# A delta net's block inverse issued in one row on VectorE, with low parts of weights moved to GpSimd meanwhile

## The chip, the cores and the metric

The kernel runs on one core of a Trainium2 chip. A core has TensorE (matmuls, with a queue of weight loads of its own), VectorE, ScalarE, GpSimd, and SyncE, which issues most of the DMAs. In the profile's rows they are PE, PEld, DVE, ACT, POOL and SP. The metric is the time of one execution on the device in microseconds (us).

## The reference

The reference is a trunk of four blocks on a sequence of 1024 tokens of 1024 features: a gated delta net, a feed-forward block with a convolution, a retention, and a second feed-forward block. Only the delta net is touched. Cut to what matters here, it is:

```python
proj = h @ w_in                                   # q, k, v, z, a, b
qkv = silu(causal_dwconv(qkv, conv_w))            # 4 taps
q, k, v = chunks of 64 tokens, 8 heads of 128     # q and k normalised
kk = where(strict, (k * beta) @ k.T * decay, 0)
sol = solve_triangular(kk + eye, [v * beta, k * beta * exp(gc)])
qk = where(causal, q @ k.T * decay, 0)
# a scan over the chunks: state and output from sol, q, k, qk
o = o * rsqrt(mean(o * o) + eps) * norm_w * silu(z)
return o @ w_out
```

The kernel treats two chunks of 64 as one chunk of 128 tokens, 8 of them, and computes the inverse of `kk + eye` for each head and chunk instead of a solve: first of its diagonal blocks of 32x32, then by matmuls of larger blocks.

## The kernel before, in words

**The stage.** The delta net's features, inverses and scan lie at about 90 to 658 us of the span. A generator per job issues its instructions: `filler` (L1028), `t_front`, `t_solve` (L766), `t_chain`, `prep`, `dt_half` (L911) and `scan`. The planner `run` (L627) holds a model clock `clk` that each matmul advances by its cost, and always resumes the job of the best priority among those that are due. A job yields a number (it is due so many us later; the numbers are in the table `LAT`), or the name of an event that another job announces with `emit`. TensorE's matmuls and transposes (`pm`, `ptr`, L616 and L619) are pinned to the order in which the planner issues them. On the other engines the framework orders the instructions from the priorities in which they were issued and from when their inputs and buffers are ready by its own model; the result is one fixed queue per engine.

**The filler.** It has the last priority and keeps TensorE busy. For each 128 columns of the projection it loads a weight tile (128x1024, 512 KB) with `load_w` (L100): a DMA brings `wr`, ScalarE copies it to the rounded high part `wh` (L89), and `split` subtracts that to get the low part `wl` (L90, on VectorE). Then come 48 matmuls of 128x512, 24 for each half of the sequence, and in each group of three the first one reads `wl`. There are two buffers each for `wr`, `wh` and `wl`; the two of `wr` are shared with `mvw`, the tiles of background products for later blocks (`bg_step`, `bg_ada`, L214 and L216, VectorE multiply-adds of 128x512). `conv_half` (L424) takes a projection from PSUM: ScalarE copies it to `raw` (L430) and scales it into `qkv` (L433), VectorE adds three taps (L435), ScalarE applies the silu (L436).

**The solve.** `t_solve` is done twice, for heads 0 to 3 and for heads 4 to 7. ScalarE gathers the 32x32 blocks to `X` (L773), VectorE transposes them to `Y` (L777), GpSimd sets `T` (L779, L780), and 31 steps follow, each a product into `fs` (L785) and a subtraction on `T` (L787), every one needing the one before it. Then VectorE transposes `T` to `RX` (L791), ScalarE permutes it to `TP` (L793), and VectorE transposes that to `TX` (L795). `t_chain` copies diagonal blocks out of these: `R` from `RX`, 12 copies on ScalarE (L833) and 12 on GpSimd (L835) for the two pairs of heads, and `T0` from `TX` on ScalarE (L822, 6 copies per pair of heads), and then multiplies blocks on TensorE. `dt_half` loads the decay into `DT`, multiplies q and k on TensorE in PSUM tiles named `mm`, and VectorE multiplies both (L933).

**Numbers of lines.** In the kernel after, lines from 434 on are moved by one or more: the low part stays L90, the projection is L617, the taps L436, the silu L437, the inverse L786 and L788, `RX` L790, `TP` L792, `TX` L794, the copies to `R` L835 and L837, and to `T0` L824.

Of the kernel before, what the change touches and what calls it, by code (L numbers as in the profile page):

```python
# [12 lines left out]
ALU = mybir.AluOpType  # L13
# [3 lines left out]
D = 1024  # L17
# [4 lines left out]
GH = 8  # L22
# [11 lines left out]
def trunk_kernel(ctx: ExitStack, tc, A):  # L34
    nc = tc.nc
    pe, act, dve, pool, sp = nc.tensor, nc.scalar, nc.vector, nc.gpsimd, nc.sync
# [24 lines left out]
    def mm_tile():  # L61
        return ps.tile([P, HALF], F32, tag="mm", name="mm", bufs=2)

    def sc_tile():
        return ps.tile([P, HALF], F32, tag="sc", name="sc", bufs=2)
# [26 lines left out]
    anchor = {}  # L92

    def after(key):
        return tc.issue_after(anchor[key].ins) if key in anchor else nullcontext()
# [4 lines left out]
    def load_w(src, tags=("wh", "wl"), raw="wr", eng=dve):  # L100
        wr = tl(raw, [P, D])
        anchor["w"] = sp.dma_start(wr, src)
        wh = tl(tags[0], [P, D], F32R, name="wh")
        wl = tl(tags[1], [P, D], F32R, name="wl")
        split(wh, wl, wr, eng)
        return kn(wh), kn(wl)
# [12 lines left out]
    def bg_step(tile=mm_tile):  # L119
        bg_ps[0] = tile  # L120
        if bg:
            bg.pop(0)()
# [38 lines left out]
    for k in range(KT):  # L161
        w = two("hTa", F32, "mvw")
# [261 lines left out]
    def conv_half(tile_idx, acc, half, o, prev):  # L424
        raw = tl("cv", [P, 516], name="raw")
        if half == 0:
            pool.memset(raw[:, 0:3], 0.0)
        else:
            pool.tensor_copy(raw[:, 0:3], prev[:, HALF:HALF + 3])
        act.activation(raw[:, 3:515], acc, AF.Copy)  # L430
        w = gdn_cw[:, tile_idx * 4:tile_idx * 4 + 4]
        oh = o[half]
        act.activation(oh, acc, AF.Copy, scale=w[:, 3:4])  # L433
        for j in range(1, 4):
            dve.scalar_tensor_tensor(oh, raw[:, 3 - j:515 - j], w[:, 3 - j:4 - j], oh, ALU.mult, ALU.add)  # L435
        act.activation(oh, oh, AF.Silu)  # L436
        return raw  # L437

# [3 lines left out]
    def ssq_tile(ti, tr):  # L442
        o = feats[ti]
        r = ssq[ti] = ct(f"ssq{ti}", [P, NCH])
        for half in range(2):
            pt = acc_tile()
            sq = tl("cv", [P, 516], name="sq")
            for c in range(4):
                cs = slice(c * P, (c + 1) * P)
                tr(pt[:, cs], o[half][:, cs])  # L450
            for c in range(4):
                n = half * 4 + c
                cs = slice(c * P, (c + 1) * P)
                act.activation(sq[:, cs], pt[:, cs], AF.Square, accum_out=r[:, n:n + 1])
        if ti < GH:
            dve.tensor_scalar(r, r, 1e-6, 1e-6 * P, ALU.add, ALU.mult)
        else:
            dve.tensor_scalar(r, r, 1e-6, None, ALU.add)
# [162 lines left out]
    def after_ev(*names):  # L621
        return ("ev", names)

    def emit(name, lat=0.0):
        events[name] = clk[0] + lat
# [50 lines left out]
    def give(tag, n):  # L676
        free[tag] += n
# [88 lines left out]
    def t_solve(qd_):  # L766
        yield after_ev(("T0", 2 * qd_ - 1), ("A", 2 * qd_), ("A", 2 * qd_ + 1))
        yield from take("lane", 1)
        X = tl("lane", [P, 32, 32], name="X")
        for h in pairs[2 * qd_] + pairs[2 * qd_ + 1]:  # L770
            for b in range(4):
                bs = slice(32 * b, 32 * b + 32)
                act.activation(X[bs, :, h % 4 * 8:h % 4 * 8 + 8].rearrange("p i c -> p c i"), U[h][bs, :, bs], AF.Copy)  # L773
        yield from take("lane", 2)
        yield LAT["X"]
        Y = tl("lane", [P, 32, 32], name="Y")
        dve.transpose(flat(Y), flat(X))  # L777
        T = tl("lane", [P, 32, 32], name="T")
        pool.memset(T, 0.0)  # L779
        pool.memset(flat(T)[:, 0:1024:33], 1.0)  # L780
        tmp = tl("fs", [P, 256], name="fs")
        for j in range(31):
            ni, nj = 31 - j, j + 1
            tv = tmp[:, 0:ni * nj].rearrange("p (i j) -> p i j", j=nj)
            dve.tensor_tensor(tv, bc(Y[:, j + 1:, j], nj), bm(T[:, j, 0:nj], ni), ALU.mult)  # L785
            ts_ = T[:, j + 1:, 0:nj]  # L786
            dve.tensor_tensor(ts_, ts_, tv, ALU.subtract)  # L787
            if j % 2:  # L788
                yield LAT["fs"]
        RX = tl("lane", [P, 32, 32], name="RX")  # L790
        dve.transpose(flat(RX), flat(T))  # L791
        TP = tl("lane", [P, 32, 32], name="TP")  # L792
        act.activation(TP, T.rearrange("p i j -> p j i"), AF.Copy)  # L793
        TX = tl("lane", [P, 32, 32], name="TX")  # L794
        dve.transpose(flat(TX), flat(TP))  # L795
        RTX[qd_] = (RX, TX)
        give("lane", 1)
        emit(("Tq", qd_))
        emit(("T", qd_), LAT["T"])
# [111 lines left out]
    def dt_half(p, q4):  # L911
        heads = pairs[p]
        if q4 == 0:
            yield after_ev(("Tq", p // 2), ("M", p - 1))
            yield from take("lane", 1)
            t = tl("lane", [P, 2, HALF], name="DT")
            tiles = [t[:, 0], t[:, 1]]
        else:
            yield after_ev(("Tq", p // 2), ("S", p - 1))
            yield from take("auh", 2)  # L920
            emit(("Dt", p))
            tiles = [tl("auh", [P, HALF], name="DT") for _ in range(2)]
        for h, t in zip(heads, tiles):
            DT[h, q4] = t
            sp.dma_start(t, Ld[h][:, hs(q4)])
        yield LAT["ld"]
        for h, t in zip(heads, tiles):
            yield after_ev(("f", h))
            pt = mm_tile()
            for c in range(4):  # L930
                n = q4 * 4 + c
                pm(pt[:, c * P:(c + 1) * P], fx(GH + h, n), fx(h, n))
            dve.tensor_tensor(t, t, pt, ALU.mult)  # L933
            emit(("D", h, q4), LAT["D"])
            yield LAT["mm"]
# [84 lines left out]
    kept = {}  # L1020
    zd = dr.tile([GH, P, S], F32, tag="zd", name="zd")

    def ssq_late(ti):
        yield LAT["ssq"]
        ssq_tile(ti, ptr)
        emit(("f", ti), 1.0)

    def filler(items):  # L1028
        spare = [(z, k) for k in range(GH)]
        todo = list(items)  # L1030
        while todo or spare:
            if not todo or (todo[0][0] == "c" and free["qkv"] < 2 and len(spare) > 4):
                kind, ti = spare.pop(0)
            else:
                kind, ti = todo.pop(0)
            if kind == "h":
                if ti > 1:
                    acc = acc_tile()
                    for k in range(KT):
                        mm3(acc, ws[ti], k, hT[1][k], k == 0, k == KT - 1, pm)  # L1040
                        yield 0.0
                    first_out(ti, 1, acc)
                if first[ti] < GH:
                    yield [(0.2, ssq_late(first[ti]))]
                else:
                    emit(("f", first[ti]), LAT["fv"])
                continue
            w = load_w(A["gdn_wqkv" if kind == "c" else "gdn_wz"][ti])
            prev = None
            if kind == "c":  # L1050
                feats[ti] = []
            for half in range(2):
                if kind == "c":
                    yield from take("qkv", 1)
                acc = acc_tile()
                for k in range(KT):
                    mm3(acc, w, k, hT[half][k], k == 0, k == KT - 1, pm)
                    yield 0.0
                if kind == "c":
                    feats[ti].append(tl("qkv", [P, HALF], name="qkv"))  # L1060
                    prev = conv_half(ti, acc, half, feats[ti], prev)
                else:
                    cv = tl("cv", [P, 516], name="sg")
                    act.activation(cv[:, 0:HALF], acc, AF.Silu)  # L1064
                    act.dma_start(zd[ti, :, hs(half)], cv[:, 0:HALF])
            if kind == "c":
                if ti < GH:
                    yield [(0.2, ssq_late(ti))]
                else:
                    emit(("f", ti), LAT["fv"])  # L1070
            bg_step(acc_tile)

    LAT = {"kk": 3.05, "ld": 1.14, "g1": 17.30, "gm": 2.50, "mm": 1.81, "T": 4.98, "X": 3.38, "fs": 1.9, "T0": 5.00, "t1": 1.65, "t2": 2.35, "t3": 1.34, "D": 2.67, "s1": 1.60, "s2": 1.22, "s3": 1.26, "tail": 12.31, "ssq": 9.30, "fv": 2.85}
    pairs = [(2 * p, 2 * p + 1) for p in range(GH // 2)]
    for nm in ("S", "T0", "Dt", "M", "Tq"):
        events[nm, -1] = 0.0
# [848 lines left out]
```

## Time and profile before

| | us |
|---|---|
| median of three runs | 3008.86 |
| the three runs | 3005.67, 3008.86, 3013.61 |
| profiled execution | 3004.66 |
| its span | 3002.8 |
| TensorE busy | 2834.6 (94%) |
| VectorE busy | 2197.4 (73%) |
| ScalarE busy | 1348.8 (45%) |
| GpSimd busy | 604.6 (20%) |

The span is the time that the trace of the profiled execution covers; its mean granted TensorE clock is 0.979 of full speed. In a row of the timeline the first number is the start in us from the beginning of the span, the second the duration of the instructions named, and the brackets at the end hold the idle time in front of them and what ended it. A row of grouped instructions ends in their count, the sum of their time in us, the mean of one in ns, and the idle time in front of them.

### The profile page before, as it was taken

How to read it: one execution, taken by the hardware profiler on the slowest of the kernel's cores; microseconds unless marked ns; L12 is line 12 of the kernel's file. 1: busy time of each engine (PE TensorE's matmuls, PEld its weight loads, DVE VectorE, ACT ScalarE, POOL GpSimd, SP SyncE). 2: the span in 40 equal slices, each digit the busy share in tenths (PEclk: the TensorE clock that was granted, in tenths of full speed). 3: DMA queues.
4: the chain of work that ended last, by engine and by line, in shares of the span. 5: the costliest groups of instructions: out<-in, count | busy, mean ns of one | idle time of the engine just before them, and what ended most of it. 6: DMA issues, size and time to landing. Idle time of an engine off the chain costs nothing.

```text
span 3002.8 us, 38880 instructions
## 1 busy us (share of the span) xinstructions
PE 2834.6 (94%) x13638; PEld 2307.8 (77%) x13638; DVE 2197.4 (73%) x3877; ACT 1348.8 (45%) x2513; POOL 604.6 (20%) x629
## 2 busy tenths in 40 slices
PE   8889998999989999999999989999999899999997
PEld 7768877887778788777787777767777678888785
DVE  5785687545687888997677765666687787778888
ACT  4655555434644444536443332221345544445444
POOL 0410311133011111620002330322201011113503
PEclk9999999999999999999999999999999999999998
DMA  7222222344344444864424463556663233336652
GB/s 272 88 75 71 95 88 64 117 158 137 109 140 161 161 155 147 305 203 127 154 82 147 158 216 110 166 169 184 197 235 129 99 133 106 105 106 216 230 172 105
DMA packets 235379, 442.35 MB, mean 147 GB/s; under 512 B 22192, under 2 KB 75696, under 8 KB 235184
## 3 DMA queue, kind: packets, MB, share of 16 engines
q1 hardware_dynamic: 205024, 387.96, 39.2%
q10 hardware_dynamic: 25152, 34.61, 3.2%
q0 software_dynamic: 5008, 17.30, 1.5%
q8 instruction: 107, 1.75, 0.2%
q14 instruction: 88, 0.72, 0.1%
HBM read 331.26 MB, written 108.53 MB: 146 GB/s over the span
## 4 chain that ended last, share of the span: by engine, by line
PE 61%; DVE 16%; issue 9%; DMA 7%; ACT 4%; POOL 2%; SPq 0%; POOLq 0%; ACTq 0%; DVEq 0%
PE acc L616 15%; PE acc L1401 7%; PE acc L1138 7%; PE acc L110 4%; PE acc L111 4%; PE acc L112 4%; PE sc L616 4%; PE sc L1138 3%; PE mm L616 2%; PE sc L1401 2%; DVE ab L90 1%; DVE bb L90 1%; PE sc L111 1%; PE sc L110 1%; PE sc L112 1%
## 5 line engine op out<-in xcount | busy, mean ns | idle before, releaser
L1401 PE MATMUL acc<-bb,ab 128*128 128x512 f32 x1800 | 431.9, 393 | 7.7 <-DVE bb L90 5.6
L1401 PEld LDWEIGHTS acc<-bb,ab 128*128 128x128 f32 x1800 | 337.3, 189 | 84.3 <-DVE bb L90 9.8
L616 PE MATMUL acc<-hT,wh 128*128 128x512 f32 x960 | 302.4, 396 | 0.0
L1539 POOL TENSOR_TENSOR o<-o 128x512 f32<-128x512 f32 x88 | 118.6, 1359 | 720.7 <-DVE o L1532 713.8
L1138 PE MATMUL acc<-T,wb 128*128 128x512 f32 x840 | 207.5, 397 | 12.5 <-DVE wb L90 12.4
L616 PEld LDWEIGHTS acc<-hT,wh 128*128 128x128 f32 x960 | 184.4, 192 | 34.5
L616 PE MATMUL acc<-hT,wl 128*128 128x512 f32 x480 | 204.6, 426 | 0.2 <-ACT sg L1064 0.2
L90 DVE TENSOR_TENSOR ab<-ar,ab 128x512 fp32r<-128x512 f32 x210 | 178.3, 857 | 28.7 <-ACT ab L89 28.6
L1138 PEld LDWEIGHTS acc<-T,wb 128*128 128x128 f32 x840 | 159.7, 191 | 50.0 <-DVE wb L90 16.7
L89 ACT ACTIVATE ab<-ar 128x512 fp32r<-128x512 f32 x210 | 128.4, 623 | 134.2 <-PE acc L1401 72.4
L90 DVE TENSOR_TENSOR wb<-wr,wb 128x512 fp32r<-128x512 f32 x162 | 113.3, 704 | 84.4 <-ACT wb L89 82.0
L90 DVE TENSOR_TENSOR wl<-wr,wh 128x1024 fp32r<-128x1024 f32 x85 | 104.2, 1226 | 96.6 <-ACT wh L89 96.6
L89 ACT ACTIVATE wh<-wr 128x1024 fp32r<-128x1024 f32 x101 | 106.8, 1058 | 127.4 <-PE acc L616 56.5
L90 DVE TENSOR_TENSOR wb<-mm,wb 128x512 fp32r<-128x512 f32 x216 | 145.0, 684 | 21.0 <-ACT wb L89 19.0
L89 ACT ACTIVATE wb<-mm 128x512 fp32r<-128x512 f32 x216 | 122.7, 594 | 76.7 <-DVE mm L1184 76.2
L1197 ACT ACTIVATE pc<-acc 128x512 f32<-128x512 f32 x143 | 84.8, 593 | 157.5 <-PE acc L1138 105.1
L89 ACT ACTIVATE wb<-wr 128x512 fp32r<-128x512 f32 x162 | 98.5, 626 | 99.7 <-DMA wr<-in_ffn_up 49.8
L616 PE MATMUL acc<-wh,hT 128*128 128x512 f32 x384 | 137.0, 419 | 2.7 <-DVE vv L90 1.6
L1518 DVE SCALAR_TENSOR_TENSOR o<-g,vc,o 128x512 f32<-128x512 f32 (+2 forms) x176 | 135.7, 789 | 1.3 <-ACT o L1513 0.6
L435 DVE SCALAR_TENSOR_TENSOR qkv<-raw,vc,qkv 128x512 f32<-128x512 f32 x144 | 114.7, 800 | 27.6 <-ACT qkv L433 26.4
L89 ACT ACTIVATE bb<-Br 128x512 fp32r<-128x512 f32 x120 | 74.0, 624 | 125.5 <-DVE Br L1285 64.3
L216 DVE SCALAR_TENSOR_TENSOR ada<-mvw,e,ada 128x512 f32<-128x512 f32 x140 | 106.9, 763 | 28.1 <-DMA mvw<-in_ada_w 27.9
(620 smaller groups left out, 7118.8 us busy)
## 6 DMA issues: line engine op xcount, KB each, us to landing
wr<-in_ffn_up SPq DMA_DIRECT2D x96, 512.0 KB, 4.2
mvw<-in_ada_w SPq DMA_DIRECT2D x80, 512.0 KB, 4.4
ad<-o SPq DMA_DIRECT2D x154, 256.0 KB, 2.3
ar<-ad SPq DMA_DIRECT2D x154, 256.0 KB, 3.8
Br<-in_ffn_down SPq DMA_DIRECT2D x66, 256.0 KB, 3.9
wr<-in_ret_wv SPq DMA_DIRECT2D x32, 512.0 KB, 3.7
ar<-od SPq DMA_DIRECT2D x56, 256.0 KB, 3.8
xs<-xt ACTq DMA_DIRECT2D x24, 512.0 KB, 3.0
```

What stands on the lines that cost most here:

```text
L89: act.activation(dst_h, src, AF.Copy)
L90: eng.tensor_tensor(dst_l, src, dst_h, ALU.subtract)
L110: mm(acc, wl[:, k], hl[0], start=first, stop=False)
L111: mm(acc, wh[:, k], hl[1], start=False, stop=False)
L112: mm(acc, wh[:, k], hl[0], start=False, stop=last)
L216: dve.scalar_tensor_tensor(a, wr[:, kk], e[:, k:k + 1], a, ALU.mult, ALU.add)
L435: dve.scalar_tensor_tensor(oh, raw[:, 3 - j:515 - j], w[:, 3 - j:4 - j], oh, ALU.mult, ALU.add)
L616: pq(pe.matmul(out, lhsT, rhs, start=start, stop=stop, **kw), cost)
L1138: return pe.matmul(*a, skip_group_check=True, **kw)
L1401: mm_ = (lambda *a, p=p, onto=onto, **kw: (mm if p < 2 else pe.matmul)(*a, skip_group_check=onto, **kw))
L1518: dve.scalar_tensor_tensor(tv, gv[:, c0 - j:c1 - j], w[:, 2 - j:3 - j], tv, ALU.mult, ALU.add)
L1539: pool.tensor_tensor(o[d], o[x], o[y], op)
```

## The change

The 62 operations of an inverse are issued without a pause: `t_solve` no longer yields between steps. Each of them becomes the anchor "inv", and what `conv_half` and `bg_step` issue under `after("inv")`, the three taps and the background products, is placed behind the last such operation on its engine. When `t_solve` has issued an inverse it enters it in the list `inverting` and yields 27.0 us (`LAT["inv"]`); the list is emptied when the planner resumes it. While the list isn't empty, the filler's `load_w` gives the low part to GpSimd in place of VectorE. Features are announced by a job of its own, `featured`: where an inverse is under way, it waits for the inverse's event and 8.0 us (`LAT["catch"]`). The scores' product in `dt_half` takes a PSUM tile of `sc_tile` in place of `mm_tile` for the first half of every other pair of heads.

```diff
         act.activation(oh, acc, AF.Copy, scale=w[:, 3:4])
-        for j in range(1, 4):
-            dve.scalar_tensor_tensor(oh, raw[:, 3 - j:515 - j], w[:, 3 - j:4 - j], oh, ALU.mult, ALU.add)
+        with after("inv"):
+            for j in range(1, 4):
+                dve.scalar_tensor_tensor(oh, raw[:, 3 - j:515 - j], w[:, 3 - j:4 - j], oh, ALU.mult, ALU.add)
         act.activation(oh, oh, AF.Silu)
...
             ts_ = T[:, j + 1:, 0:nj]
-            dve.tensor_tensor(ts_, ts_, tv, ALU.subtract)
-            if j % 2:
-                yield LAT["fs"]
+            anchor["inv"] = dve.tensor_tensor(ts_, ts_, tv, ALU.subtract)
...
         RTX[qd_] = (RX, TX)
+        inverting.append(("Tq", qd_))
+        yield LAT["inv"]
+        inverting.clear()
         give("lane", 1)
         emit(("Tq", qd_))
...
-            pt = mm_tile()
+            pt = mm_tile() if p % 2 or q4 else sc_tile()
...
-    def ssq_late(ti):
-        yield LAT["ssq"]
-        ssq_tile(ti, ptr)
-        emit(("f", ti), 1.0)
+    inverting = []
+
+    def featured(ti):
+        if inverting:
+            yield after_ev(inverting[0])
+            yield LAT["catch"]
+        if ti < GH:
+            yield LAT["ssq"]
+            ssq_tile(ti, ptr)
+            emit(("f", ti), 1.0)
+        else:
+            emit(("f", ti), LAT["fv"])
...
-                if first[ti] < GH:
-                    yield [(0.2, ssq_late(first[ti]))]
-                else:
-                    emit(("f", first[ti]), LAT["fv"])
+                emit(("f", first[ti]), LAT["fv"])
                 continue
-            w = load_w(A["gdn_wqkv" if kind == "c" else "gdn_wz"][ti])
+            w = load_w(A["gdn_wqkv" if kind == "c" else "gdn_wz"][ti], eng=pool if inverting else dve)
...
             if kind == "c":
-                if ti < GH:
-                    yield [(0.2, ssq_late(ti))]
-                else:
-                    emit(("f", ti), LAT["fv"])
-            bg_step(acc_tile)
+                yield [(0.2, featured(ti))]
+            with after("inv"):
+                bg_step(acc_tile)
...
+    LAT = {..., "inv": 27.0, "catch": 8.0, ...}
```

The framework's order of the instructions changes with it. The first place is GpSimd's queue at the first inverse. In the kernel before, from the scale `ir` of the last head, over the setting of `T` and the edges of `raw`, to the copies of `R`, it holds:

```order
L759 TENSOR_TENSOR ir_1297<-sk_1295,phalf_82 128x8
L779 MEMSET T_1463 128x1024
L780 MEMSET T_1463 128x32
L429 COPY raw_1540<-raw_1472 128x3
L427 MEMSET raw_1593 128x3
L429 COPY raw_1661<-raw_1593 128x3
L427 MEMSET raw_1717 128x3
L429 COPY raw_1759<-raw_1717 128x3
L427 MEMSET raw_1915 128x3
L835 COPY R_1866<-RX_1796 32x4x32 x2
L835 COPY R_1867<-RX_1796 32x4x32 x2
```

In the kernel after, the rows from the third edge of `raw` on are these, where `wl_1686` and `wl_1764` are the low parts of the third and fourth weight tile that the filler loads while the inverse is under way:

```order
L429 COPY raw_1671<-raw_1637 128x3
L837 COPY R_1823<-RX_1529 32x4x32 x2
L837 COPY R_1824<-RX_1529 32x4x32 x2
L837 COPY R_1835<-RX_1529 32x4x32 x2
L837 COPY R_1836<-RX_1529 32x4x32 x2
L837 COPY R_2461<-RX_1529 32x4x32 x2
L837 COPY R_2462<-RX_1529 32x4x32 x2
L820 MEMSET T0_1814 32x8x32 x2
L427 MEMSET raw_1715 128x3
L90 TENSOR_TENSOR wl_1686<-wr_1683,wh_1685 128x1024
L90 TENSOR_TENSOR wl_1764<-wr_1761,wh_1763 128x1024
```

One low part, `wl_1608` of the second tile, stands ahead of the setting of `T`; the next two stand behind the 12 copies to `R`, which read `RX`. Before, no low part was on GpSimd here.

The second place is ScalarE's queue at the same inverse. Before, these rows stand around the permutation `TP`; `wh_1773` and `wh_2081` are high parts of weight tiles:

```order
L89 ACTIVATE wh_1773<-wr_1771 128x1024
L430 ACTIVATE raw_1717<-acc_1679 128x512
L433 ACTIVATE qkv_1716<-acc_1679,vc_153 128x512
L436 ACTIVATE qkv_1660<-qkv_1660 128x512
L436 ACTIVATE qkv_1716<-qkv_1716 128x512
L430 ACTIVATE raw_1759<-acc_1725 128x512
L433 ACTIVATE qkv_1758<-acc_1725,vc_153 128x512
L89 ACTIVATE wh_2081<-wr_2079 128x1024
L436 ACTIVATE qkv_1758<-qkv_1758 128x512
L793 ACTIVATE TP_1798<-T_1463 128x1024
L833 ACTIVATE R_1866<-RX_1796 32x4x32 x2
```

After, the row of the permutation stands behind the second tile's last projection, and these follow:

```order
L433 ACTIVATE qkv_1670<-acc_1645,vc_153 128x512
L792 ACTIVATE TP_1531<-T_1463 128x1024
L835 ACTIVATE R_1823<-RX_1529 32x4x32 x2
L835 ACTIVATE R_1824<-RX_1529 32x4x32 x2
L835 ACTIVATE R_1835<-RX_1529 32x4x32 x2
L835 ACTIVATE R_1836<-RX_1529 32x4x32 x2
L835 ACTIVATE R_2461<-RX_1529 32x4x32 x2
L835 ACTIVATE R_2462<-RX_1529 32x4x32 x2
L824 ACTIVATE T0_1814<-TX_1533 32x8x32 x6
L437 ACTIVATE qkv_1535<-qkv_1535 128x512
L89 ACTIVATE wh_1685<-wr_1683 128x1024
```

The third tile's high part `wh_1685` stands behind `TP`, 12 copies to `R`, 6 to `T0` and a silu; the silus of the projections between have moved behind the inverse, with their taps. On TensorE, the last projection matmuls of the second tile and the first of the third are neighbours in the kernel after:

```order
L617 MATMUL acc_1645<-hT_658,wl_1608 128x512
L617 MATMUL acc_1645<-hT_658,wh_1607 128x512 x2
L617 MATMUL acc_1645<-hT_674,wl_1608 128x512
L617 MATMUL acc_1645<-hT_674,wh_1607 128x512 x2
L617 MATMUL acc_1689<-hT_280,wl_1686 128x512
L617 MATMUL acc_1689<-hT_280,wh_1685 128x512 x2
```

TensorE has no other instruction between them. At the second inverse GpSimd makes `wl_4020` ahead of the copies, and `wl_4098` and `wl_4176` stand behind them in the same way.

More of the change, by code (lines that the diff above doesn't have):

```diff
@@ L1066, in filler @@
             if kind == "c":
-                if ti < GH:
-                    yield [(0.2, ssq_late(ti))]
-                else:
-                    emit(("f", ti), LAT["fv"])
-            bg_step(acc_tile)
-    LAT = {"kk": 3.05, "ld": 1.14, "g1": 17.30, "gm": 2.50, "mm": 1.81, "T": 4.98, "X": 3.38, "fs": 1.9, "T0": 5.00, "t1": 1.65, "t2": 2.35, "t3": 1.34, "D": 2.67, "s1": 1.60, "s2": 1.22, "s3": 1.26, "tail": 12.31, "ssq": 9.30, "fv": 2.85}
+                yield [(0.2, featured(ti))]
+            with after("inv"):
+                bg_step(acc_tile)
+    LAT = {"kk": 3.05, "ld": 1.14, "g1": 17.30, "gm": 2.50, "mm": 1.81, "T": 4.98, "X": 3.38, "inv": 27.0, "catch": 8.0, "T0": 5.00, "t1": 1.65, "t2": 2.35, "t3": 1.34, "D": 2.67, "s1": 1.60, "s2": 1.22, "s3": 1.26, "tail": 12.31, "ssq": 9.30, "fv": 2.85}
     pairs = [(2 * p, 2 * p + 1) for p in range(GH // 2)]
```

## The prediction

> **What bounds the kernel now.** I read first the page (TensorE busy for 94% of the span), then the time windows around the two inverses of the delta net, then the waits, then the timelines of each engine there. Which stage limits this change is answered by the windows:
>
> ```profile
> 175.00:205.00 30.00, 29.14 (x141) 24.06 (x139) 27.39 (x60) 15.70 (x50) 0.95 (x5) 1.00 0.30 88
> 205.00:228.00 23.00, 9.52 (x52) 7.94 (x53) 17.68 (x40) 10.12 (x19) 5.26 (x14) 0.75 0.14 46
> ...
> 425.00:480.00 55.00, 42.55 (x213) 35.75 (x212) 49.92 (x109) 27.50 (x79) 7.81 (x20) 0.90 0.30 96
> 480.00:505.00 25.00, 25.00 (x301) 20.74 (x300) 14.54 (x29) 13.38 (x21) 1.10 (x4) 0.95 0.21 65
> 505.00:658.00 153.00, 147.32 (x1024) 127.13 (x1023) 80.10 (x177) 67.39 (x169) 26.19 (x25) 0.99 0.36 119
> ```
>
> The columns are the window, its length, the busy time of TensorE, weight loads, VectorE, ScalarE and GpSimd (each with its instructions), the granted clock, and DMA. TensorE has work nearly all the time except in two places: in 205 to 228 it is idle for 23.00 - 9.52 = 13.5 us, in 425 to 480 for 55.00 - 42.55 = 12.4 us. The clock is lost there too:
>
> ```profile
> 216.40:230.00 13.60, 6.06 (x22) 5.25 (x23) 7.55 (x15) 10.74 (x19) 5.26 (x14) 0.50 0.11 39
> ```
>
> Here 6.06 us of matmuls run at 0.50, so they take 3.0 us more than at full clock. What ends the idle time is seen in the waits of 170 to 230 us and in TensorE's timeline:
>
> ```profile
> POOL R L835 <- DVE RX L791: 23.9, 1, 23.9
> ACT TP L793 <- DVE T L787: 11.5, 1, 11.5
> ...
> PE mm L616 <- DVE DT L933: 11.1, 1, 11.1
> ```
>
> ```profile
> 176.22 0.47 PE L616 MATMUL acc<-hT,wl 128*128 128x512 f32 x1
> ...
> 223.94 2.08 PE L616 MATMUL mm<-qkv 128*128 128x128 f32 x8 [11.08 <-DVE DT L933]
> ...
> 416.95 0.48 PE L616 MATMUL acc<-hT,wl 128*128 128x512 f32 x1
> ...
> 438.83 0.39 PE L616 MATMUL acc<-hT,wl 128*128 128x512 f32 x1
> ...
> 477.50 2.07 PE L616 MATMUL mm<-qkv 128*128 128x128 f32 x8 [9.38 <-DVE DT L933]
> ...
> 657.69 0.61 PE L616 MATMUL acc<-hT,wh 128*128 128x512 f32 x2
> ```
>
> VectorE, which carries the inverse, the taps and the low parts, is what TensorE waits for; no DMA ends these waits. The last row is a projection matmul at the stage's very end, at 657.69: since the same matmuls fill TensorE until then in both kernels, an idle microsecond that is taken away (or added) at the inverses moves the end of the stage.
>
> **The inverse in a row.** Before, the 62 operations of an inverse are spread out between taps and background products:
>
> ```profile
> 169.21 1.22 DVE L90 TENSOR_TENSOR wl<-wr,wh 128x1024 fp32r<-128x1024 f32 x1
> 170.34 0.75 DVE L435 SCALAR_TENSOR_TENSOR qkv<-raw,vc,qkv 128x512 f32<-128x512 f32 x1
> 171.00 0.75 DVE L216 SCALAR_TENSOR_TENSOR ada<-mvw,e,ada 128x512 f32<-128x512 f32 x1
> 172.19 1.25 DVE L777 STREAM_TRANSPOSE Y<-X 128x1024 f32<-128x1024 f32 x1 [0.44 <-ACT X L773]
> ...
> 218.06 0.19 DVE L787 TENSOR_TENSOR T<-T,fs 128x31 f32<-128x31 f32 x1
> 218.28 1.25 DVE L791 STREAM_TRANSPOSE RX<-T 128x1024 f32<-128x1024 f32 x1
> ```
>
> ```profile
> 170.00:225.00 55.00, 10.53 (x31) 0.92 0.25 77
> ```
>
> ```profile
> 170.00:225.00 55.00, 10.58 (x31) 0.92 0.25 77
> ```
>
> ```profile
> 212.39:218.25 5.86, 0.46 (x5) 0.27 (x3) 5.27 (x18) 0.00 (x0) 0.00 (x0) 0.84 0.00 1
> ```
>
> The rows with 55.00 are the windows of L785 and of L787 alone (length, VectorE's busy time, clock, DMA); they sum to 21.1 us. The last one is the end of the first inverse, where 18 of its operations already stand in a row: (5.86 - 5.27)/18 = 0.033 us from one to the next. So 62 in a row take 21.1 + 2.0 = 23.1 us, where they took 218.28 - 173.44 = 44.8 from the lead-in's end. The transpose that leads in (172.19) stands behind a low part and a background product (169.21 and 171.00) that the new order has elsewhere. So it starts between 172.19 - 1.97 = 170.2 and 172.19; I take 170.2. The first inverse then ends at E1 = 170.2 + 1.25 + 23.1 + 0.2 (one small operation in the row, an estimate) = 194.8. In the second, three taps stand inside the row (0.66 us each, 171.00 - 170.34), and its lead-in is in place as before:
>
> ```profile
> 422.63 1.25 DVE L777 STREAM_TRANSPOSE Y<-X 128x1024 f32<-128x1024 f32 x1 [0.88 <-ACT X L773]
> ```
>
> E2 = 423.9 + 23.1 + 2.0 = 449.0. By itself this is 218.3 - 194.8 = 23.5 us of gain for the chain of the solve, and I would forecast faster if TensorE had work in the meantime.
>
> **The low parts on GpSimd: where TensorE stops.** It doesn't have work. By the rows of the new order, GpSimd makes one low part ahead of the inverse, and then come 12 copies R<-RX that wait for the inverse, and behind them the third and the fourth low part. On ScalarE the third weight's high part stands behind TP, 12 copies R, 6 copies T0 (a copy of TX) and a silu. These queues run in order: before, GpSimd sat 23.9 us in that wait (the row above) and did nothing else. TensorE in its order has 3 + 48 projection matmuls from 176.22 on in the first inverse, 96 from 416.95 in the second, and then one that reads the low part that is missing. A projection matmul takes (438.83 - 416.95)/96 = 0.228 us. TensorE stops at 176.22 + 51 x 0.228 = 187.9, and at 438.8.
>
> A rule of the Trainium skill bears on this ("Perfetto Trace Analysis", section "Tensor Engine Instruction (MATMUL, LD_WEIGHTS)"): ScalarE, VectorE and GpSimd are strict first-in-first-out, only TensorE's weight loads may pass others. The trace agrees by the 23.9 us; were it otherwise, rival A would be the forecast.
>
> **When it goes on.** The chain from the inverse's end E to the third low part is made of these:
>
> ```profile
> 218.28 1.96 ACT L793 ACTIVATE TP<-T 128x1024 f32<-128x1024 f32 x1 [11.46 <-DVE T L787]
> 220.15 5.12 ACT L833 ACTIVATE R<-RX 32x128 f32<-32x128 f32 x12
> 225.29 3.97 ACT L822 ACTIVATE T<-TX 32x256 f32<-32x256 f32 x6
> ```
>
> ```profile
> 219.66 5.23 POOL L835 COPY R<-RX 32x128 f32<-32x128 f32 x12 [23.94 <-DVE RX L791]
> ```
>
> ```profile
> L90 POOL TENSOR_TENSOR wl<-wr,wh 128x1024 fp32r<-128x1024 f32 x16 | 38.9, 2430 | 54.1 <-ACT wh L89 52.8 <-issue 1.2
> ```
>
> ```profile
> L89 ACT ACTIVATE wh<-wr 128x1024 fp32r<-128x1024 f32 x29 | 30.8, 1063 | 0.0
> L436 ACT ACTIVATE qkv<-qkv 128x512 f32<-128x512 f32 x45 | 28.5, 632 | 51.3 <-DVE qkv L435 51.0
> ```
>
> Three operations stand between the inverse and RX (two taps, one background product, at most 0.66 us each): RX ends at E + 2.0 + 1.2 = E + 3.2. ScalarE's R copies 5.1: E + 8.3; T0 copies 4.0: E + 12.3; silu 0.6: E + 12.9; high part 1.1: E + 14.0; GpSimd's low part 2.4: E + 16.4. GpSimd's own R copies end at E + 8.4, inside this. The weight's DMA waits for a buffer that VectorE's next background product frees:
>
> ```profile
> wr<-in_gdn_wqkv SPq DMA_DIRECT2D x15, 512.0 KB, 3.5
> ```
>
> That product stands behind two taps, TX and one more tap, and ends at about E + 7.7, so the tile lands at about E + 11, also inside. TensorE goes on at 194.8 + 16.4 = 211.2 and at 449.0 + 16.4 = 465.4. It is idle 211.2 - 187.9 = 23.3 us where it was 13.5, and 465.4 - 438.8 = 26.6 where it was 12.4: +9.8 and +14.2.
>
> **The clock.** In both kernels TensorE starts again after a long idle time in each solve, so the 3.0 us that a restart loses stands on both sides. The Trainium skill's rule ("TensorE: Matmul & The Clock Gate", section "What's actually happening") is that one idle window of about 3.4 us halves the clock and about 3.4 us of work restores it, which loses 1.7 us a restart (an estimate from that page): by it rival A would gain 2 x 1.3 = 2.6 us less, and the forecast stays; the row shows 3.0.
>
> **The other edits.** The low parts off VectorE (1.22 us each) and the taps put behind it gain nothing for TensorE in the inverse, since TensorE waits for GpSimd there. The taps and products come back in a block of 17 operations behind TX, 11 us at 0.66, from E + 6 to E + 17; they delay the DT multiplication that TensorE waits for today, but TensorE then has 48 matmuls of the third weight (10.9 us, to E + 27) ahead of it. If that cover were gone, the DT products would wait as they do today, 11.1 us at most. The fourth low part needs a free wr tile (E + 16.4), a DMA 3.5, wh 1.1, wl 2.4: E + 23.4, 4 us ahead of its use. The DT waits of 11.1 and 9.4 us are inside the idle time already counted and go. The later announcement of features and the scores' PSUM tile for a part of the DT products add no work: I take 0, with -5 to +5 for what they shift in the streams. Sum: +9.8 + 14.2 = +24.0. On the profiled execution, 3004.66 + 24.0 = 3028.7; the runs' median, 3008.86, is 4.2 above that execution, so I forecast 3033.
>
> **The rivals.** About 0.3%, 9 us, is what a measurement of this kernel can tell from no change.
>
> A, the other side: the third and fourth low parts come in time, so that TensorE works through both inverses. This needs the low part at 187.9, 6.9 us ahead of E1, on a queue whose head waits for E1. Then both idle times and two restarts go: 13.5 + 12.4 + 2 x 3.0 = 31.9, 3008.9 - 31.9 = 2977. For it speaks only that the work for TensorE is there; the order and the 23.9 us speak against. It decides where the low part comes earlier than 13.5 us after the stop. Chance 0.09.
>
> B: the chain is shorter than I make it (R copies on GpSimd and ScalarE end at E + 8.4, and the high part could be there sooner if a copy or the DMA were not in its way), or what the stall costs is given back later, because the solve's chain is 23 us earlier and the 5.4 us of idle time between 350 and 400 or the 5.7 us between 505 and 658 shrink:
>
> ```profile
> 350.00:400.00 50.00, 44.65 (x234) 37.10 (x233) 39.59 (x121) 28.04 (x44) 15.54 (x21) 0.93 0.32 110
> ```
>
> Giving back 11 us and having chains 5 us shorter, the change is +24.0 - 11 - 10 = +3, about 3012. Chance 0.14.
>
> C: the fourth low part is late as well: its 4 us are gone if the wr tile comes later or GpSimd is slowed beside VectorE's block of taps. Each microsecond is then paid twice, once per solve; at 5 us beyond them, +24 + 10, about 3043. Chance 0.12.
>
> **How the numbers follow.** Forecast 0.65, A 0.09, B 0.14, C 0.12. The forecast's own bounds: the lead-in at 172.19 instead of 170.2 is +2, the shifts -5 to +5, three shorter operations in front of RX -1 each: 3022 to 3040. The range that holds 8 in 10 goes from part of B to C: 3009 to 3044. Faster by over 0.3% (below 2999.8): A and a little of B, 0.10. Within 0.3% (to 3017.9): most of B, 0.14. Slower: 0.76.
>
> **What would show it.** Right: TensorE has one idle time of 20 us or more in each solve, from about 188 and 439 us, ended by the low part L90 on GpSimd; the last inverse operation is at about 195 and 449; GpSimd's R copies end some 8 us behind it; the stage's last projection matmul is at about 682. Wrong at the step of the queues: a low part on GpSimd between the two blocks of the inverse. Wrong at the size: idle time below 18 us. Wrong in the sum: idle times as forecast, but the end of the stage moved by much less.

## The result, and the profile after

Six runs of the changed kernel have a median of 3034.28 us (3028.83 to 3041.79), six of the kernel before 3008.31 us (3002.30 to 3013.61): a ratio of 1.0085, 95% interval 1.0067 to 1.0103, or +25.6 us. The forecast was 3033. The profiled execution takes 3028.83 us where that of before takes 3004.66: +24.2.

The waits of all engines between 165 and 245 us (total, times, longest), and TensorE's timeline at its two long waits and at the end of the stage:

```profile
PE acc L617 <- POOL wl L90: 23.9, 1, 23.9
...
POOL R L837 <- DVE RX L790: 15.1, 1, 15.1
```

```profile
210.34 0.79 PE L617 MATMUL acc<-hT,wl 128*128 128x512 f32 x1 [23.88 <-POOL wl L90]
...
476.84 0.80 PE L617 MATMUL acc<-hT,wl 128*128 128x512 f32 x1 [27.93 <-POOL wl L90]
...
685.68 1.05 PE L1562 MATMUL mm<-dg,ones 128*128 128x128 f32 x8
```

The wait of TensorE for the scores' multiplication (11.1 and 9.4 us before) is gone, and one for a low part on GpSimd is in its place, two to three times as long. The row at 685.68 is the first matmul of the next stage, which stood at 658.14: +27.5 us. The windows of the two waits, and then those of the stage (90 us to that matmul), after and before, with the columns of the prediction's windows:

```profile
185.85:210.34 24.49, 0.61 (x3) 0.19 (x2) 21.44 (x42) 15.23 (x26) 11.47 (x16) 0.60 0.16 51
...
448.50:477.00 28.50, 0.57 (x3) 0.16 (x1) 23.47 (x50) 14.70 (x25) 11.43 (x15) 0.59 0.17 55
```

```profile
90.00:685.68 595.68, 516.90 (x3486) 440.69 (x3485) 398.91 (x945) 303.20 (x658) 138.62 (x171) 0.94 0.27 88
```

```profile
90.00:658.14 568.14, 520.54 (x3493) 441.20 (x3492) 393.59 (x955) 302.18 (x658) 120.35 (x167) 0.96 0.28 93
```

TensorE is idle for 595.68 - 516.90 = 78.8 us of the stage where it was 568.14 - 520.54 = 47.6. These 31.2 us more of idle time, less the 3.6 by which the busy time is shorter, are the 27.5 us.

The inverse itself is what the diff says, in a row. VectorE's timeline (lead-in, the last operations of the first inverse, `RX`), then ScalarE's, GpSimd's and SyncE's around the first wait:

```profile
169.37 1.23 DVE L778 STREAM_TRANSPOSE Y<-X 128x1024 f32<-128x1024 f32 x1
...
194.04 0.19 DVE L788 TENSOR_TENSOR T<-T,fs 128x31 f32<-128x31 f32 x1
...
195.87 1.24 DVE L790 STREAM_TRANSPOSE RX<-T 128x1024 f32<-128x1024 f32 x1
...
201.05 0.88 DVE L216 SCALAR_TENSOR_TENSOR ada<-mvw,e,ada 128x512 f32<-128x512 f32 x1
```

```profile
197.14 5.18 ACT L835 ACTIVATE R<-RX 32x128 f32<-32x128 f32 x12 [0.81 <-DVE RX L790]
202.33 3.92 ACT L824 ACTIVATE T<-TX 32x256 f32<-32x256 f32 x6
206.27 0.63 ACT L437 ACTIVATE qkv<-qkv 128x512 f32<-128x512 f32 x1
206.81 1.04 ACT L89 ACTIVATE wh<-wr 128x1024 fp32r<-128x1024 f32 x1
```

```profile
197.23 8.97 POOL L837 COPY R<-RX 32x128 f32<-32x128 f32 x12 [15.10 <-DVE RX L790]
...
207.93 2.36 POOL L90 TENSOR_TENSOR wl<-wr,wh 128x1024 fp32r<-128x1024 f32 x1 [1.08 <-ACT wh L89]
215.82 2.39 POOL L90 TENSOR_TENSOR wl<-wr,wh 128x1024 fp32r<-128x1024 f32 x1 [5.53 <-ACT wh L89]
```

```profile
168.92 0.38 SPq L210 DMA_DIRECT2D mvw<-in_ada_w  x1
197.18 0.80 SPq L927 DMA_DIRECT2D DT<-Ld  x2
201.96 0.33 SPq L102 DMA_DIRECT2D wr<-in_gdn_wqkv  x1
208.11 0.38 SPq L210 DMA_DIRECT2D mvw<-in_ada_w  x1
```

The inverse ends at E = 194.2 and GpSimd has made the third low part at E + 16.1. The SyncE rows show something that the prediction named only in passing: from 169 to 197 us no DMA is issued, and none of a weight until 201.96. That is just behind the end of a background product, 201.05 + 0.88 = 201.93. A product's tile `mvw` uses one of the two `wr` buffers, and the product now has to wait behind the inverse. In fact both buffers are held through it, by the tiles of two products (loaded at 132.63 and 168.92): the next `mvw`, at 208.11, goes out as the second product ends (208.08).

SyncE's queue has one more link. Its waits between 155 and 240 us hold these two:

```profile
SPq L927 <- DVE RX L790: 27.8, 1, 27.8
...
SPq L102 <- DVE ada L216: 3.9, 1, 3.9
```

The transfer of the decay, `DT`, stands ahead of the weight in this queue and waits 27.8 us for `RX`; the weight's own wait for the product is only the 3.9 us behind it. So the weight is late by its place in SyncE's queue, as the high part is by its place in ScalarE's. Why it has this place is what the experiments have to tell.

### The profile page after: what moved, and what is told of

Read it like the earlier page. It is cut to its first block, busy times and chain, and to the rows that moved or that the text cites. A ratio compares the mean times of both kernels' runs of the same rounds, so it can differ in the third digit from the quotient of the medians.

```text
span 3026.8 us, 38871 instructions
## 1 busy us (share of the span) xinstructions
PE 2829.1 (93%) x13638; PEld 2307.2 (76%) x13638; DVE 2207.4 (73%) x3871; ACT 1349.8 (45%) x2515; POOL 622.4 (21%) x635
## 4 chain that ended last, share of the span: by engine, by line
PE 57%; DVE 16%; issue 9%; DMA 9%; ACT 5%; POOL 2%; SPq 0%; POOLq 0%; ACTq 0%; DVEq 0%
PE acc L617 14%; PE acc L1143 7%; PE acc L1406 6%; PE acc L110 4%; PE acc L111 4%; PE acc L112 4%; PE sc L1143 3%; PE sc L617 3%; PE mm L617 2%; PE sc L1406 2%; DVE ab L90 2%; DMA wr<-in_ffn_up 1%; PE sc L111 1%; PE sc L112 1%; PE sc L110 1%
## 5 line engine op out<-in xcount | busy, mean ns | idle before, releaser
L617 PE MATMUL acc<-hT,wl 128*128 128x512 f32 x480 | 204.7, 426 | 52.0 <-POOL wl L90 51.8
L90 DVE TENSOR_TENSOR wl<-wr,wh 128x1024 fp32r<-128x1024 f32 x79 | 96.6, 1223 | 96.0 <-ACT wh L89 95.7
L617 PEld LDWEIGHTS acc<-hT,wl 128*128 128x128 f32 x480 | 92.9, 194 | 67.2 <-POOL wl L90 52.7
L436 DVE SCALAR_TENSOR_TENSOR qkv<-raw,vc,qkv 128x512 f32<-128x512 f32 x144 | 119.4, 839 | 31.2 <-ACT qkv L433 30.0
```

Of the source, the lines that this page charges most:

```text
L90: eng.tensor_tensor(dst_l, src, dst_h, ALU.subtract)
L617: pq(pe.matmul(out, lhsT, rhs, start=start, stop=stop, **kw), cost)
```

## The experiments

Two theories stood at the start. **The held buffer**: background products hold the `wr` buffers until the inverse is done; the third weight can't be loaded, and that its DMA, its high part and its low part stand late in their queues only follows from it. **GpSimd**: its queue and its slower subtraction make the low part late (rival 1). A third says that taps and products, packed behind the inverse, cost as much as the row gains, wherever they stand (rival 2). All ratios are to the kernel before on the same chip; "stage end" is the first matmul of the next stage in the profiled execution, 658.1 before and 685.7 with the change.

| run | median us | ratio, 95% interval | stage end |
|---|---|---|---|
| e1_products_free | 3014.52 | 1.0013 (0.9999 to 1.0027) | 672.7 |
| e2_low_on_vector | 3033.42 | 1.0081 (1.0059 to 1.0103) | 689.4 |
| e3_products_later | 3018.65 | 1.0036 (1.0019 to 1.0052) | 673.3 |
| e4_small_edits | 3021.24 | 1.0035 (1.0023 to 1.0047) | 670.0 |
| e5_owed_behind | 3022.51 | 1.0042 (1.0028 to 1.0056) | 678.7 |
| e6_owed_two | 3006.11 | 0.9999 (0.9984 to 1.0014) | 658.1 |
| e7_owed_vector | 3020.39 | 1.0032 (1.0017 to 1.0047) | 672.8 |
| e8_scores_tile | 3025.54 | 1.0056 (1.0032 to 1.0079) | 671.0 |
| e9_owed_late | 3003.64 | 0.9984 (0.9965 to 1.0003) | 658.4 |
| e10_owed_late_mm | 3008.86 | 0.9993 (0.9976 to 1.0010) | 656.9 |
| e11_change_mm | 3039.56 | 1.0102 (1.0081 to 1.0124) | 693.1 |
| e12_before_low_gpsimd | 3023.62 | 1.0056 (1.0035 to 1.0077) | 674.8 |

### e1: the products issued freely

```diff
-            with after("inv"):
-                bg_step(acc_tile)
+            bg_step(acc_tile)
```

> The changed kernel with the background products issued as before, without after("inv"); all else stays. Theory (the background tile holds one of the two wr buffers until the inverse is done, so that the third weight can't be loaded, and the queues of ScalarE and GpSimd are ordered behind that): the third and fourth low parts come on GpSimd while the inverse is under way, the idle times of 23.9 and 27.9 us shrink to under 6 us each, and the time is 2978 to 2996 us. Rival 1 (the late part is GpSimd's slow subtraction and its queue): the idle times stay at 18 us or more, 3020 us or above. Rival 2 (the row and the block of taps behind it cost by themselves): idle times go but come back behind the inverse, 3008 us or above.

GpSimd's timeline of this run, then TensorE's:

```profile
184.92 2.59 POOL L90 TENSOR_TENSOR wl<-wr,wh 128x1024 fp32r<-128x1024 f32 x1 [2.96 <-ACT wh L89]
...
194.87 2.73 POOL L90 TENSOR_TENSOR wl<-wr,wh 128x1024 fp32r<-128x1024 f32 x1 [6.71 <-ACT wh L89]
216.06 7.94 POOL L837 COPY R<-RX 32x128 f32<-32x128 f32 x12 [18.46 <-DVE RX L790]
```

```profile
221.93 0.80 PE L617 MATMUL mm<-T,U 32*32 32x32 f32 x16 [4.37 <-ACT T L824]
...
482.32 0.79 PE L617 MATMUL acc<-hT,wl 128*128 128x512 f32 x1 [12.53 <-ACT ada L228]
```

That one line undone, the third and fourth low parts come at 184.9 and 194.9, during the inverse, and both waits for a low part are gone. In SyncE's queue three weights now go out at 175.06, 182.96 and 195.04, ahead of `DT` at 216.01. So the products' place behind the inverse is the cause of the two waits. That the buffer is the link is not yet shown by this run alone; e5 shows it below. The ratio falls from 1.0085 to 1.0013, by some 20 us, but not to the 2978 to 2996 us that were expected: products, a low part and other work are inside the inverse again, and `RX` comes at 214.7 (36.5 us behind the lead-in's end). Other waits take the place: in the first solve 4.37 us for `T0`, in the second 12.53 us for the last step of a block of background products (L228). Rival 1 falls; the sign of rival 2 (idle times that come back, 3008 us or above) came.

### e2: the low parts on VectorE

```diff
-            w = load_w(..., eng=pool if inverting else dve)
+            w = load_w(..., eng=dve)
```

> The changed kernel with all low parts on VectorE again, the products still behind the inverse. Theory (the held wr buffer): the third weight's DMA still waits for the first product behind the inverse, so the third low part is ready about 14 us behind the inverse's end whichever engine makes it; idle times of 22 to 29 us, 3024 to 3040 us. Rival 1 (GpSimd's queue and its slower subtraction): the low part comes 3 to 5 us behind the inverse's end, idle times of about 14 us, 3006 to 3016 us.

TensorE's waits of this run between 90 and 680 us:

```profile
PE acc L617 <- DVE wl L90: 48.6, 2, 25.8
```

The same two waits, 48.6 us in place of 51.8, with another engine's name. GpSimd is not what makes the low part late.

### e3, e5, e6, e9: the products paid later

In all four, a product that falls due during an inverse is owed, and takes no tile yet. e3 pays all at the next weight, without `after`; e5 the same with `after("inv")`; e6 two at each weight; e9 two at each weight, from one weight later on. The edit of e9 is shown (`owed` and `hold` start as `[0]`); e6's expectation starts from e5.

```diff
-            with after("inv"):
-                bg_step(acc_tile)
+            owed[0] += 1
+            with after("inv"):
+                hold[0] = 2 if inverting else max(hold[0] - 1, 0)
+                for _ in range(0 if hold[0] else min(owed[0], 2)):
+                    owed[0] -= 1
+                    bg_step(acc_tile)
```

> The changed kernel, in which no background product is issued while an inverse is under way; those owed are issued at the next weight after it. Theory (the held wr buffer): the weights load all through the inverse, idle times under 6 us, 2975 to 2994 us, at most 5 us from the kernel with the products issued freely. Rival 2 (row and taps cost by themselves): 3008 us or above. If products inside the inverse matter for its length, this is 3 to 8 us faster than with products issued freely.

> The changed kernel, in which no background product is issued while an inverse is under way and those owed are issued after it, all at once, with after("inv"): the row stays clean of products and the wr buffers are free for weights. Theory (the held buffer made the idle time; what was left of it with the products free came from what stood inside the inverse, which took 36 us): the inverse ends 28 to 30 us after its start, TensorE works on to about 210 us, idle time per solve 5 to 12 us, 2990 to 3008 us. Rival 2 (taps and products behind the inverse cost as much as the row gains, wherever they stand): 3012 us or above.

> As the run before in this call, but the owed products are paid back two at each weight in place of all at once. Theory: the fifth weight isn't held back by four products, so this is 2 to 8 us faster than all at once, 2985 to 3004 us. Rival 2: the same time as all at once, 3012 us or above.

> The changed kernel, in which the products owed from the inverse are paid back two at a time, beginning one weight later than in the run that paid two at once (3006 us). There the fifth weight waited in the second solve for a wr buffer that two products held, 14.1 us. Theory: that wait goes, 2990 to 3002 us. Rival 2 (the block behind the inverse costs the same wherever it stands): 3003 us or above.

All waits of TensorE for a low part in e5 between 90 and 700 us, then its longest wait in the second solve of e5, that of e6, and all its waits in e9 between 457 and 480 us:

```profile
PE acc L617 <- DVE wl L90: 3.0, 2, 1.5
```

```profile
484.83 1.09 PE L226 MATMUL acc<-cst,ada 128*128 128x128 f32 x4 [16.82 <-DVE ada L216]
```

```profile
470.21 0.80 PE L617 MATMUL acc<-hT,wl 128*128 128x512 f32 x1 [14.13 <-DVE wl L90]
```

```profile
466.41 0.82 PE L617 MATMUL mm<-T,U 32*32 32x32 f32 x16 [3.23 <-ACT T L824]
468.40 2.58 PE L617 MATMUL mm<-T,U 32*32 32x32 f32 x48 [1.17 <-ACT T L824]
...
476.67 0.21 PE L617 MATMUL mm<-R,xa 32*32 32x32 f32 x1 [2.41 <-ACT xa L851]
```

e5 tells the buffer from the place. Its products stand behind the inverse as in the change, but no tile was taken for them while it was issued. The third and fourth low parts come at 184.7 and 194.7 during the first inverse, at 437.7 and 448.6 during the second, and no wait for a low part is longer than 1.5 us. So it was the tiles that the products held, and not their place on VectorE. No run gave the products buffers of their own.

e3 and e5 missed all the same, and in different ways. In e5 all four products are paid at once, and TensorE waits 16.82 us for the last step behind them. In e3 nothing keeps the products behind the inverse, and the framework put them into it, from 189 us on: `RX` starts at 213.1, and the longest wait is again one for L228 (11.87 us), as in e1. The row is worth nothing in either (1.0036 and 1.0042). In e6 two products hold both buffers ahead of the fifth weight, and its low part is 14.13 us late: the mechanism of the change once more, one weight further on. e6 missed its range by 2 us. In e9 that wait is gone as expected. From e5 over e6 to e9 the ratio went from 1.0042 to 0.9999 to 0.9984, the last step within noise. But e9 was expected at 2990 to 3002 us and came out at 3003.64, where rival 2 has its bound of 3003; its interval holds no change, and its stage ends where it did before.

The windows of the second solve from 455 to 505, of e9 and then of before, show where the gain goes:

```profile
455.00:505.00 50.00, 40.07 (x351) 35.05 (x350) 37.27 (x62) 31.68 (x78) 10.63 (x22) 0.76 0.27 85
```

```profile
455.00:505.00 50.00, 37.55 (x375) 31.56 (x374) 36.09 (x76) 27.19 (x64) 7.80 (x20) 0.86 0.24 75
```

TensorE is idle for 9.9 us in place of 12.4, but at a granted clock of 0.76 in place of 0.86. Where before there was one long wait (9.38 us) and full speed again some 5 us behind its end, there now are short waits at each link (`T0` copies, `xa`, `R`), and the clock falls again and again. The window of the whole stage of e9 says the same:

```profile
90.00:658.43 568.43, 529.70 (x3501) 452.29 (x3500) 405.96 (x952) 305.81 (x662) 142.15 (x174) 0.95 0.28 93
```

TensorE is idle for 38.7 us in place of 47.6, and busy for 529.7 us in place of 520.5: slower matmuls take back what the waits gave. This fits that e9 gains nothing; it was read from one profiled execution, and no run changed it alone.

### e7: GpSimd's worth where the weights flow

The kernel of e5 with `eng=dve` for all low parts.

> As the first run of this call, with all low parts on VectorE. Where weights flow, this tells GpSimd's worth: if GpSimd's low part holds up VectorE for 2.1 us each, as two rows of the runs so far show, the inverse is 1 to 2 us shorter per solve with the low parts on VectorE (1.2 us each), and the time 2 to 5 us less than in the first run. If GpSimd relieves VectorE as it is meant to, the time is 3 to 8 us more.

The intervals of e5 and e7 overlap (1.0042 and 1.0032), and `RX` starts 29.9 and 31.1 us behind the lead-in's end in e5's two solves, 31.5 and 29.8 in e7's. Inconclusive: neither a gain nor a loss of GpSimd can be told here.

### e12: GpSimd's low parts in the kernel before

```diff
-            w = load_w(A["gdn_wqkv" if kind == "c" else "gdn_wz"][ti])
+            w = load_w(A["gdn_wqkv" if kind == "c" else "gdn_wz"][ti], eng=pool)
```

> The kernel before with all low parts of the delta net's weights on GpSimd. If a low part on GpSimd holds up VectorE for 2.1 us, as two rows show, against 1.2 us that VectorE needs for it, the inverses end later by 1 us per low part made meanwhile, 3 to 4 us per solve, and the time is 3008 to 3022 us; if it relieves VectorE, the inverses end 4 to 5 us earlier and the time is 2996 to 3004 us.

The windows of L785 alone (the inverse's products on VectorE) in the first solve, of e12 and then of before:

```profile
170.00:230.00 60.00, 17.11 (x31) 0.79 0.22 70
```

```profile
170.00:230.00 60.00, 10.53 (x31) 0.89 0.23 71
```

The same 31 operations take 6.6 us more, beside three low parts on GpSimd: 2.2 us for each, where VectorE needs 1.2 us to make one itself. In the second solve L785 is as fast as before (10.51 us), and the hold-ups fall on other operations of VectorE: on a tap (2.83 us), a product (2.55) and one subtraction on `T` (2.57). From the lead-in's end to `RX` the two inverses take 4.1 and 4.0 us more than before, as was expected of a hold-up. The kernel is 0.56% slower, some 16 us and just above the range. The two inverses account for about half; the edit moves every low part of the stage, and where the rest arises was not looked for. VectorE isn't relieved: in the stage it is busy for 406.3 us in place of 393.6, though its low parts there went from 37.4 us to 3.9.

### e4, e8, e10, e11: the small edits

e8 is the kernel before with the scores' tile of the change alone, e4 that and the announcing by a job of its own; e10 and e11 are e9 and the changed kernel with the tile of before.

```diff
-            pt = mm_tile()
+            pt = mm_tile() if p % 2 or q4 else sc_tile()
```

> The kernel before with only the small edits: announcing by a job of its own and the scores' tile from the other PSUM pool; the inverse is spread out again, with no anchor, no 27 us and all low parts on VectorE. All theories: within 6 us of the kernel before, 3002 to 3015 us. If these edits carried the loss, 3025 us or above.

> The kernel before with the scores' PSUM tile of the change alone. The small edits together took 11 us: if the tile carries it, 3017 to 3024 us here; if the announcing does, 3005 to 3012 us.

> As the run before in this call, with the scores' tile from mm_tile as in the kernel before. The tile alone took 16 us where the inverse is spread out, since it moved TensorE's wait from the scores to the first products with T0, at a later inverse. With the inverse in a row that wait is small, so that the tile should matter less: within 6 us of the run before in this call. If the tile costs by itself, 10 us or more faster.

> The changed kernel with the scores' tile from mm_tile as before, all else as changed. Theory (the time goes in the two waits for the low part, ahead of any scores): within 6 us of the changed kernel, 3027 to 3040 us. Rival (the tile carries most of the loss, as alone): 3015 to 3022 us.

TensorE's timeline and VectorE's in the first solve of e8:

```profile
232.33 1.06 PE L616 MATMUL mm<-T,U 32*32 32x32 f32 x16 [17.68 <-ACT T L822]
```

```profile
224.64 1.25 DVE L791 STREAM_TRANSPOSE RX<-T 128x1024 f32<-128x1024 f32 x1
```

e4 missed: the small edits that were to cost nothing cost 11 us in the kernel before, and the tile alone 17 (1.0056). e8 came out just above its range. With the tile, TensorE no longer stops for the scores (11.1 us), and more work reaches VectorE: between 172 and 218 us it does 21 taps in place of 18 and 49 of the inverse's operations in place of 61. The spread-out inverse ends 6.4 us later (`RX` at 224.6, 218.3 before), and TensorE waits 17.7 us for the first product with `T0`. In the changed kernel the tile decides nothing: undone, it is 1.0102 where the change is 1.0085, with the two waits as they were (51.8 us), and e10 is within noise of e9. So the loss of the change is not that of the tile. Announcing wasn't tried alone.

No version beat the kernel before by more than its interval. So rival 2 stands as a forecast of the time, though the wait in which it is paid differs from run to run.

## Why the prediction was right, point by point

**Where TensorE stops.** Right. Forecast 187.9, measured 210.34 - 23.88 = 186.5, as the projections begin 1.6 us earlier (the same marker at 174.61 in place of 176.22). In the second solve 438.8 and the 9.8 us by which the first solve was forecast to be late make 448.6; measured 476.84 - 27.93 = 448.9.

**The inverse.** Right: E1 forecast 194.8, measured 194.2. The second ran in a row too and took 25.1 us as forecast, but from 436.1 to 461.2 and not to 449.0: the prediction's times for the second solve leave out the delay of the first.

**When it goes on.** Right link by link: `RX` E + 3.2 (measured 2.9), ScalarE's copies to `R` E + 8.3 (8.1) and to `T0` E + 12.3 (12.0), high part E + 14.0 (13.6), low part E + 16.4 (16.1). Idle 23.9 and 27.9 us where 23.3 and 26.6 were forecast. One sign was off: GpSimd's copies to `R` end at E + 12.0 and not E + 8.4, since they took 8.97 us beside the taps; this was inside ScalarE's part of the chain and cost nothing.

**The sum.** +24.0 forecast on the profiled execution, +24.2 measured. That it fits so well is luck in part. The two waits added 25.9 us and not 24.0; other idle time of the stage added 5.3, for which the sum has no term but its -5 to +5; the busy time fell by 3.6. So the stage's end moved by 27.5 us. Behind the stage the profiled execution is 3.4 us shorter than before; over all the runs that part lies between 2343 and 2356 us. A restart lost 2.1 and 1.9 us (the first 4.66 us behind the one wait had a mean clock of 0.54, 8.00 us behind the other 0.76) where 3.0 was taken on both sides.

**One reading.** The sentence "no DMA ends these waits" holds for TensorE's own rows. But before, the multiplication of `DT` that ended TensorE's wait had itself waited for a DMA, which had stood 15.3 us in SyncE's queue until `TP` of the inverse was done:

```profile
223.19 0.69 DVE L933 TENSOR_TENSOR DT<-DT,mm 128x512 f32<-128x512 f32 x1 [1.67 <-DMA DT<-Ld]
```

**The cause.** Here the step was incomplete. The prediction put the stop down to the low part's place behind GpSimd's 12 copies, and to ScalarE's copies ahead of the high part. ScalarE's part is what binds in the trace: it works without a pause from `R` at 197.14 to the high part's end at 207.85. GpSimd's copies were done in time (the low part's own wait is 1.08 us, for the high part), and with the low part on VectorE the wait stayed (e2). The weight's DMA is inside the chain as forecast: issued at 201.96, and 3.5 us at the median to land, it is there before the high part starts at 206.81. What the prediction didn't ask is where the order comes from. The tiles of background products, which `after("inv")` put behind the inverse, held the buffers that the weight needs. Where the tiles don't hold them, the same framework puts both low parts ahead of the copies (e1, e5).

**The other edits.** The forecast took 0 for the scores' tile. That holds in the changed kernel (e11), but not because it adds no work: alone it costs 17 us, by moving TensorE's wait to a later link.

**GpSimd's low part.** That it gains nothing for TensorE was right and too mild. In the kernel before it holds VectorE up for longer than the work it takes away (e12); where the weights flow, e5 and e7 can't tell.

**The rivals.** A needed the low part early and priced that at 31.9 us. e9 gives the low part early and gains nothing that its interval can tell (0.9965 to 1.0003), so that this price was far too high: by the profile, the solve's later links take the place of the wait, at a lowered clock. B's give-back didn't show. C's fourth low part came at E + 24.0 (forecast 23.4), and TensorE did not wait for it.

## What to carry to other kernels

When work is put behind a barrier, list the buffers that it holds while it waits, and who else draws from the same pool: here a background tile of no urgency kept the critical weights out. A low part or a copy that stands late in a queue may only stand there because its input was planned late; moving it to another engine then changes the name in the waits and not the time, as in e2. And where a long wait is taken away from a chain, price the next link before counting the gain, with the clock that TensorE has when it works in short pieces.

## What the runs showed of the hardware

**GpSimd's low part stops VectorE.** VectorE's timeline of e1, beside GpSimd's rows at 184.92 and 194.87 (2.59 and 2.73 us long) that are shown above:

```profile
185.29 2.44 DVE L786 TENSOR_TENSOR fs<-Y,T 128x192 f32<-128x192 f32 x1
187.76 0.36 DVE L788 TENSOR_TENSOR T<-T,fs 128x192 f32<-128x192 f32 x1
...
195.38 2.51 DVE L786 TENSOR_TENSOR fs<-Y,T 128x256 f32<-128x256 f32 x1
197.92 0.43 DVE L788 TENSOR_TENSOR T<-T,fs 128x256 f32<-128x256 f32 x1
```

An operation of the inverse that begins beside GpSimd's subtraction ends 0.2 to 0.3 us behind it, after 2.44 us where the same operation took 0.36 in the changed kernel, and after 2.51 where it took 0.42. The other way round, GpSimd's 12 copies to `R` took 8.97 us beside VectorE's block of taps where they took 5.23 before. The Trainium skill has this rule ("SBUF — State Buffer", section "SBUF: two separate sides"): VectorE and GpSimd share a port pair that one of them holds for a whole instruction, also where VectorE's operation has two inputs in SBUF and GpSimd's reads SBUF. The rows agree: the inverse's operations and the taps have two such inputs. The prediction left the rule out.

**Short waits lower the clock too.** In e9 no wait of TensorE between 455 and 505 us is longer than 3.23 us, and yet the mean granted clock there is 0.76. These windows stand around the wait of 2.41 us that ends at 476.67:

```profile
475.00:477.00 2.00, 0.33 (x20) 0.33 (x22) 2.00 (x4) 1.95 (x4) 0.00 (x0) 1.00 0.50 190
477.00:479.00 2.00, 2.00 (x75) 2.00 (x69) 2.00 (x3) 0.61 (x2) 0.00 (x0) 0.51 0.08 11
479.00:481.00 2.00, 2.00 (x22) 1.94 (x21) 2.00 (x4) 0.64 (x2) 0.00 (x0) 0.50 0.84 240
```

The clock is halved just behind this wait, while TensorE is busy. The Trainium skill ("TensorE: Matmul & The Clock Gate", section "What's actually happening") asks for one idle window of about 3.4 us to halve the clock; the run shows the loss with shorter waits between small products.
